# A scheduling priority, 400 instructions ahead, for the recurrence of a hybrid encoder block

## The chip, the cores and the metric

The kernel runs on one core of one Trainium2 chip. The metric is the time of one execution in device microseconds. A core has five engines that this document names: TensorE (PE in the profile, with PEld for its weight loads), VectorE (DVE), ScalarE (ACT), GpSimd (POOL) and SyncE (SP), which here only issues DMAs. Each engine works through its own queue in order; engines wait for each other by semaphores.

## The reference

One encoder layer on a sequence of 1024 tokens, model width 1024, all in float32:

```python
h = rms_norm(x, norm_mix_g)
q, pc, pr = split(h @ w_in)
o = concat([memory_cross_attention(q, mem_n), conformer_conv(pc), rwkv7_bidirectional(pr)])
x = x + o @ w_out
x = x + expert_choice_ffn(rms_norm(x, norm_ffn_g))   # 16 experts, 128 tokens each
y = rms_norm(x, final_norm_g)
```

What matters here is the third group, a recurrence over the tokens with a 64x64 state for each of 6 heads, run once forward and once backward:

```python
def step(state, inp):
    r_t, w_t, k_t, v_t, kk_t, a_t = inp
    sa = einsum('bhij,bhj->bhi', state, -kk_t)
    state = state * w_t[..., None, :] + sa[..., :, None] * (kk_t * a_t)[..., None, :] + v_t[..., :, None] * k_t[..., None, :]
    return state, einsum('bhij,bhj->bhi', state, r_t)
```

## The kernel before, in words

The program has three parts. Up to some 380 us it multiplies the normed input with `w_in` and does the convolution and the cross-attention. From there to some 840 us runs the recurrence, with the first five eighths of the product with `w_out` laid under it (`residual`) and the last part of that product and of the router behind it (`out56`, `partial`). From 860 us on come the experts, which this change does not touch.

The recurrence is cut into chunks of 64 tokens. Six units u = 0 to 5 follow each other: three pairs of heads, two halves each, and a unit holds 8 chunk steps for both directions and both heads of a pair at once. For each unit three things are prepared before its chain can run:

- `prep` (L775) makes the decayed keys and queries (tiles AR, BK): on DVE L801 to L826, on ACT L793 to L814.
- `within` (L845) multiplies them chunk by chunk into the tiles AM (PE L854, masked on DVE at L857).
- `invert` (L887) inverts a triangular matrix per chunk. ACT copies AM into Ld (L895), DVE turns it (L900), and then 31 rounds of two DVE instructions each, L910 (dtmp) and L911 (Dt), depend on one another in a row. After that DVE turns the result back (L916, Dr), ACT and DVE make TT of it (L921, L922), DVE turns a part once more (L926, D), PE multiplies (L934), ACT copies (L938, W), PE multiplies (L945), ACT copies (L949). Then TT is ready.

`chain` (L954) is the recurrence itself. One step of it goes round four engines: PE multiplies the state S0 and the values SV into psX (L969, L971), DVE copies that to Xs (L973), PE multiplies it with TT into psSA (L981), DVE and ACT copy half of that each into SV (L982, L983), PE multiplies into psS (L988), and DVE adds two products into the next state (L991, twice). POOL makes the decayed old state (L965, sps). Beside that PE adds eight products per step to the outputs psY (L976, L996). The first step of unit u needs TT of unit u, at L981, and the state that unit u-1 left.

What sets the order is a generator planner, `run` (L224), that interleaves the functions as the program is recorded, and behind it a scheduler that fills each engine's queue: where several instructions are ready for an engine, the one recorded earlier goes first. The planner's windows (R_INV, R_P and the like, L60 to L93) put `invert`, `prep` and `within` of unit u+1 between the steps of chain u.

Of the kernel before, what the change touches and what calls it, by code (L numbers as in the profile page):

```python
# [12 lines left out]
F32 = mybir.dt.float32  # L13
# [3 lines left out]
ALU = mybir.AluOpType  # L17
# [3 lines left out]
P = 128  # L21
# [10 lines left out]
C = 64  # L32
# [22 lines left out]
FL = [0, 0, 0, 0, 0, 0, 0, 0]  # L55
# [28 lines left out]
NBOR = 0  # L84
PLACE = [11, 2, 3, 4, 5, 6, 7, 8, 1, 9, 10, 0]
NYE = 1
GT = 5
R_O56 = [-3, 36]
R_G2 = [-3, 22]
# [11 lines left out]
def hybrid_block_kernel(ctx: ExitStack, tc: tile.TileContext, x, xT, memT, memn, w_in, w_mk, w_mv, pcols,  # L101
                        ups, gate_up, w_out, g_ffn, g_fin, w_router, w_eg, w_eu, w_ed, out, dbg=None):
    nc = tc.nc
    V, A, G, T = nc.vector, nc.scalar, nc.gpsimd, nc.tensor
# [116 lines left out]
    def mm(tagp="mm", w=512, shape=None, name="mm", bufs=None):  # L221
        return psums[-1].tile(shape or [P, w], F32, name=name, tag=tagp, bufs=bufs or mmb[0].get(tagp))
# [80 lines left out]
    for k in range(KT):  # L303
        h = hp.tile([P, S], F32R, name=f"hh{k}")
        l = hp.tile([P, S], F32R, name=f"hl{k}")
        for n in range(2):
# [5 lines left out]
                                   op1=ALU.subtract)  # L312
# [285 lines left out]
    def attention():  # L598
        assert "kv" in ready
        for hp2 in range(2):  # L600
            for n in range(2):
                pT = at.tile([P, 4, 512], F32, name="pT", tag="pT", bufs=1)
                for jj in range(4):
# [48 lines left out]
    Z = {}  # L652
# [69 lines left out]
    lo, hi = slice(0, 64), slice(64, 128)  # L722
# [229 lines left out]
    state = [None]  # L952

    def chain(p, k, g):  # L954
        AR, BT, SV, TT, pcs = (g[n] for n in ("AR", "BT", "SV", "TT", "pcs"))
        TT = TT.rearrange("p (d c) a b -> p d c (a b)", d=2)
        if k == 0:
            state[0] = Z["sp"].tile([P, 2, C], F32, name="S0", bufs=3)
            V.memset(state[0], 0.0)
        Y = [mm(f"y{d}", shape=[P, HC, C], name="psY", bufs=1) for d in range(2)]  # L960
        for cc in range(HC):
            S0 = state[0]
            AM, c4 = [g["AM", d, cc // 4] for d in range(2)], cc % 4
            sps = Z["sp"].tile([P, 2, C], F32, name="sps", bufs=2)
            G.tensor_mul(sps, S0, pcs[:, :, cc:cc + 1].to_broadcast([P, 2, C]))  # L965
            X = mm("cx", shape=[P, 2, C], name="psX", bufs=2)
            for d in range(2):
                for h, r_, w_ in ((0, lo, hi), (1, hi, lo)):
                    T.matmul(X[w_, d], lhsT=AM[d][r_, c4, h, 0, :], rhs=SV[r_, d, cc, h, :], start=True, stop=False)  # L969
                for r_, w_ in ((lo, hi), (hi, lo)):  # L970
                    T.matmul(X[w_, d], lhsT=AR[r_, d, cc, 0, :], rhs=S0[r_, d], start=False, stop=True)  # L971
            Xs = Z["sp"].tile([P, 2, C], F32, name="Xs", bufs=2)
            (A.copy if FL[3] else V.tensor_copy)(Xs, X)  # L973
            for d in range(2):
                for r_ in (lo, hi):
                    T.matmul(Y[d][r_, cc], lhsT=S0[r_, d], rhs=AR[r_, d, cc, 1, :], start=True, stop=False)  # L976
            yield
            SA = mm("cx", shape=[P, 2, C], name="psSA", bufs=2)
            for d in range(2):
                for r_ in (hi, lo):  # L980
                    T.matmul(SA[r_, d], lhsT=TT[r_, d, cc], rhs=Xs[r_, d], start=True, stop=True)  # L981
            (A.copy if FL[4] else V.tensor_copy)(SV[hi, :, cc, 0, :], SA[hi])  # L982
            (V.tensor_copy if FL[5] else A.copy)(SV[lo, :, cc, 1, :], SA[lo])  # L983
            yield
            S1 = mm("cx", shape=[P, 2, C], name="psS", bufs=2)
            for d in range(2):
                for h, r_ in ((0, lo), (1, hi)):
                    T.matmul(S1[r_, d], lhsT=BT[:, d, cc, h, :], rhs=SV[:, d, cc, h, :], start=True, stop=True)  # L988
            Sn = Z["sp"].tile([P, 2, C], F32, name="S0", bufs=3)
            for d in range(2):  # L990
                V.scalar_tensor_tensor(Sn[:, d], S1[:, d], pcs[:, d, cc:cc + 1], sps[:, d], op0=ALU.mult,  # L991
                                       op1=ALU.add)
            state[0] = Sn
            for d in range(2):
                for h, r_ in ((0, lo), (1, hi)):
                    T.matmul(Y[d][r_, cc], lhsT=SV[:, d, cc, h, :], rhs=AM[d][:, c4, h, 1, :], start=False, stop=True)  # L996
            yield
        Y = [a.rearrange("p a b -> p (a b)") for a in Y]
        if k == 0:
            pair[p]["y"] = Z["sp"].tile([P, S], F32, name="y", bufs=1)  # L1000
        y = pair[p]["y"]
        if k == 0:
            A.copy(y[:, half(0)], Y[0])
            V.tensor_copy(y[:, half(1)][:, ::-1], Y[1])
        else:
            V.tensor_add(y[:, half(1)], y[:, half(1)], Y[0])
            V.tensor_add(y[:, half(0)], y[:, half(0)], Y[1][:, ::-1])
# [381 lines left out]
    for q, op in enumerate((ALU.is_gt, ALU.is_equal)):  # L1389
# [7 lines left out]
             start=True, stop=False)  # L1397
    T.matmul(ps.rearrange("p a b c -> p (a b c)"), lhsT=belowr, rhs=sel.rearrange("p a b c -> p (a b c)"),
             start=False, stop=False)
# [240 lines left out]
```

## Time and profile before

| | |
|---|---|
| Time, median of 3 runs | 1490.68 us (1480.89 to 1491.66) |
| The profiled execution | 1489.13 us |
| its span, first to last instruction | 1487.2 us |
| mean granted TensorE clock | 0.927 |
| PE busy | 1333.4 us, 90% |
| DVE busy | 1216.1 us, 82% |
| ACT busy | 831.2 us, 56% |
| POOL busy | 266.4 us, 18% |

Busy shares are averages over stages with different limits. A matmul's record can reach into the next one's, so a busy PE is not PE at its peak. The clock is a share of full speed, which is 2.4 GHz; the other level is 1.2 GHz. An idle stretch is put down to the engine whose instruction ended the wait.

### The profile page before, as it was taken

To read this page: it belongs to the slowest core of one execution; us is meant where nothing else is said; L and a number is where in the kernel's file an instruction comes from. 1 tells how busy PE (TensorE), PEld (TensorE's weight loads), DVE (VectorE), ACT (ScalarE), POOL (GpSimd) and SP (SyncE) were. 2 spreads that over 40 slices of the span, in tenths; PEclk is the share of its full clock that TensorE was granted. 3 is DMA by queue.
4 is the path that set the end of the run, shared out by engine and by line. 5 is a ranking of instruction groups with operands and counts; after the bars stand their busy time and mean duration, and the time that the engine had idled before them with its cause. 6 is when DMAs were issued, how large, how long until landed. Compare 5 with 4: busy or idle time off the path is not lost.

```text
span 1487.2 us, 24329 instructions
## 1 busy us (share of the span) xinstructions
PE 1333.4 (90%) x9238; PEld 1069.4 (72%) x9238; DVE 1216.1 (82%) x2120; ACT 831.2 (56%) x1214; POOL 266.4 (18%) x238
## 2 busy tenths in 40 slices
PE   6888999997888889888999719999999999999996
PEld 5777667675777776767868618888888887887773
DVE  8899975699686869696833678999999988998886
ACT  4222574433535244434322418888888877887875
POOL 2233322532120312130221000100000110110010
PEclk9999899998898888888999859999999999999998
DMA  8212112422443533342473657999999999999985
GB/s 294 71 61 67 64 64 97 152 71 73 141 143 93 157 97 117 105 121 84 142 272 142 269 198 293 386 393 390 385 385 390 381 379 344 370 377 377 370 302 201
DMA packets 146100, 327.91 MB, mean 220 GB/s; under 512 B 9792, under 2 KB 64960, under 8 KB 145984
## 3 DMA queue, kind: packets, MB, share of 16 engines
q1 hardware_dynamic: 139360, 303.14, 55.6%
q0 software_dynamic: 6192, 22.55, 5.4%
q8 instruction: 72, 1.18, 0.3%
q10 hardware_dynamic: 432, 0.68, 0.1%
q14 instruction: 44, 0.36, 0.1%
HBM read 288.58 MB, written 37.75 MB: 219 GB/s over the span
## 4 chain that ended last, share of the span: by engine, by line
PE 60%; DVE 23%; DMA 6%; ACT 5%; issue 4%; POOL 1%; SPq 0%; POOLq 0%; DVEq 0%; ACTq 0%
PE mm L330 14%; PE mm L331 14%; PE mm L329 14%; DVE cv L517 3%; DVE dtmp L910 2%; DVE Dt L911 2%; DMA fo<-oT_d 2%; PE mm L1435 2%; ACT Ld L895 2%; DMA xk<-in_xT_dram 1%; PE mm L745 1%; PE psA L854 1%; DVE ewl L1354 1%; PE mm L1165 1%; PE mm L1575 1%
## 5 line engine op out<-in xcount | busy, mean ns | idle before, releaser
L1354 DVE SCALAR_TENSOR_TENSOR ewl<-eraw,pc,ewh 128x1024 fp32r<-128x1024 f32 x256 | 315.6, 1280 | 30.5 <-ACT ewh L1353 28.4
L1353 ACT ACTIVATE ewh<-eraw,pc 128x1024 fp32r<-128x1024 f32 x256 | 283.8, 1149 | 31.7 <-PE mm L331 25.7
L330 PE MATMUL mm<-ewl,xh 128*128 128x512 f32 x512 | 202.1, 395 | 3.2 <-DVE ewl L1354 3.0
L331 PE MATMUL mm<-ewh,xl 128*128 128x512 f32 x512 | 200.1, 391 | 0.0
L329 PE MATMUL mm<-ewh,xh 128*128 128x512 f32 x512 | 190.4, 397 | 2.5 <-ACT ewh L1353 2.5
L1350 DVE TENSOR_TENSOR ewl<-eraw,ewh 128x1024 fp32r<-128x1024 f32 x120 | 139.0, 1219 | 2.8 <-ACT ewh L1349 2.8
L329 PE MATMUL mm<-hh,wh 128*128 128x512 f32 x304 | 125.4, 413 | 9.6 <-ACT hh L310 9.6
L1349 ACT ACTIVATE ewh<-eraw 128x1024 fp32r<-128x1024 f32 x120 | 121.6, 1057 | 10.6 <-PE mm L331 9.5
L331 PE MATMUL mm<-hh,wl 128*128 128x512 f32 x304 | 125.5, 413 | 0.8 <-POOL wl L325 0.8
L330 PE MATMUL mm<-hl,wh 128*128 128x512 f32 x304 | 125.1, 412 | 0.9 <-DVE hl L311 0.9
L330 PEld LDWEIGHTS mm<-ewl,xh 128*128 128x128 f32 x512 | 96.6, 189 | 25.8 <-DVE ewl L1354 7.3
L329 PEld LDWEIGHTS mm<-ewh,xh 128*128 128x128 f32 x512 | 96.1, 188 | 23.2 <-ACT ewh L1353 4.2
L331 PEld LDWEIGHTS mm<-ewh,xl 128*128 128x128 f32 x512 | 96.3, 188 | 19.7 <-DVE xl L1438 0.2
L330 PE MATMUL mm<-ewl,fh 128*128 128x512 f32 x240 | 94.6, 394 | 0.3 <-DVE ewl L1350 0.2
L331 PE MATMUL mm<-ewh,fl 128*128 128x512 f32 x240 | 93.6, 390 | 0.0
L329 PE MATMUL mm<-ewh,fh 128*128 128x512 f32 x240 | 88.0, 390 | 0.0
L325 POOL TENSOR_TENSOR wl<-wraw,wh 128x512 fp32r<-128x512 f32 x38 | 58.7, 1548 | 124.5 <-ACT wh L324 83.6
L329 PEld LDWEIGHTS mm<-hh,wh 128*128 128x128 f32 x304 | 59.6, 196 | 25.4 <-ACT hh L310 9.6
L1472 POOL DMA_INDIRECT x_d<-ye,idx x15 | 25.9, 1724 | 283.3 <-ACT ye L1471 283.3
L1420 POOL DMA_INDIRECT xe<-h_d,idx x16 | 28.9, 1805 | 247.0 <-DVE gates L1418 182.3
L517 DVE SCALAR_TENSOR_TENSOR cv<-u,cw,cv 128x512 f32<-128x512 f32 (+1 forms) x87 | 71.5, 853 | 0.1
L330 PEld LDWEIGHTS mm<-hl,wh 128*128 128x128 f32 x304 | 59.1, 194 | 17.4 <-issue 2.7
(417 smaller groups left out, 2950.7 us busy)
## 6 DMA issues: line engine op xcount, KB each, us to landing
eraw<-in_w_eg_dram SPq DMA_DIRECT2D x64, 1024.0 KB, 7.9
eraw<-in_w_eu_dram SPq DMA_DIRECT2D x64, 1024.0 KB, 9.1
eraw<-in_w_ed_dram SPq DMA_DIRECT2D x64, 1024.0 KB, 7.4
fo<-oT_d SPq DMA_DIRECT2D x64, 320.0 KB, 3.9
wraw<-in_w_in_dram SPq DMA_DIRECT2D x38, 256.0 KB, 2.8
ld_k<-d_k SPq DMA_DIRECT2D x18, 256.0 KB, 3.1
ld_v<-d_v SPq DMA_DIRECT2D x18, 256.0 KB, 3.3
xk<-in_xT_dram SPq DMA_DIRECT2D x16, 256.0 KB, 4.7
```

The lines of the kernel that those rows point to most:

```text
L325: G.tensor_sub(wl, raw, wh.bitcast(F32))
L329: T.matmul(ps, lhsT=lh, rhs=rh, start=first, stop=False)
L330: T.matmul(ps, lhsT=lh, rhs=rl, start=False, stop=False)
L331: T.matmul(ps, lhsT=ll, rhs=rh, start=False, stop=last)
L517: V.scalar_tensor_tensor(o[:, 0:ln], z, w, o[:, 0:ln], op0=ALU.mult, op1=ALU.add)
L895: A.copy(Ld[r_, :, c:c + 4].rearrange("p t c -> p c t"), g["AM", d, q][r_, :, h, 0, b * 32:b * 32 + 32])
L910: IE.tensor_tensor(tmp[:, sg, ts], lcol, drow, op=ALU.mult)
L911: IE.tensor_tensor(Dt[:, sg, ts], Dt[:, sg, ts], tmp[:, sg, ts], op=ALU.add)
L1349: A.activation(h, raw[a], AF.Copy)
L1350: V.tensor_sub(l, raw[a], h.bitcast(F32))
L1353: A.activation(h, raw[a], AF.Copy, scale=gain)
L1354: V.scalar_tensor_tensor(l, raw[a], gain, h.bitcast(F32), op0=ALU.mult, op1=ALU.subtract)
```

## The change

Everything that one chain step issues is recorded under a priority 400 instructions ahead of its place. The scheduler then picks a ready chain instruction before any other ready instruction that was recorded up to 400 places earlier. No instruction is added, taken away or changed; the instructions of each engine are the same ones in another order. Three blocks of `chain` are wrapped, with the `yield`s between them:

```diff
+AHEAD = 400
...
         for cc in range(HC):
-            S0 = state[0]
...
+            with tc.high_priority(AHEAD):
+                S0 = state[0]
...
+                (A.copy if FL[3] else V.tensor_copy)(Xs, X)
...
             yield
+            with tc.high_priority(AHEAD):
+                SA = mm("cx", shape=[P, 2, C], name="psSA", bufs=2)
...
             yield
+            with tc.high_priority(AHEAD):
+                S1 = mm("cx", shape=[P, 2, C], name="psS", bufs=2)
...
             yield
```

In the rows of the changed kernel the line numbers are 2 to 5 higher: Xs is L976 there, the SV copy L986, the state L996, Dt L913, the first turn back D L928.

The first place is DVE in unit 0, from the copy Xs of its fourth step on. Before:

```order
L973 COPY Xs<-psX 128x128
L910 TENSOR_TENSOR dtmp<-Lt,Dt 128x8x17
L911 TENSOR_TENSOR Dt<-Dt,dtmp 128x8x17
L910 TENSOR_TENSOR dtmp<-Lt,Dt 128x8x16
L911 TENSOR_TENSOR Dt<-Dt,dtmp 128x8x16
L910 TENSOR_TENSOR dtmp<-Lt,Dt 128x9x15
L911 TENSOR_TENSOR Dt<-Dt,dtmp 128x9x15
L910 TENSOR_TENSOR dtmp<-Lt,Dt 128x9x14
L1089 TENSOR_TENSOR fx<-mm,fx 128x256
L982 COPY SVa<-psSA 64x2x64
```

The same place now, from the same copy Xs on:

```order
L976 COPY Xs<-psX 128x128
L986 COPY SVa<-psSA 64x2x64
L859 TENSOR_TENSOR AM_3006<-psA,mask 128x4x128
L996 SCALAR_TENSOR_TENSOR S_3791<-psS,pcs_1922,sps 128x64 x2
L976 COPY Xs<-psX 128x128
L986 COPY SVa<-psSA 64x2x64
L996 SCALAR_TENSOR_TENSOR S_3907<-psS,pcs_1922,sps 128x64 x2
L976 COPY Xs<-psX 128x128
L986 COPY SVa<-psSA 64x2x64
L1094 TENSOR_TENSOR fx<-mm,fx 128x256
```

Where eight instructions, seven of them of unit 1's inversion, stood between two instructions of the chain, the chain now goes on for nearly three steps with one other instruction between (the mask into AM) and one behind; the inversion of unit 1 (dtmp, Dt) has moved further back.

The second place is PE in unit 0, fifth step, from its product psSA on (mm with fwh, fwl are the residual product, psA is `within`). Before:

```order
L981 MATMUL psSA<-Xs,TT_1939 64x64 x4
L329 MATMUL mm<-fwh,fo_3849 128x256
L330 MATMUL mm<-fwl,fo_3849 128x256
L331 MATMUL mm<-fwh,fo_3850 128x256
...
L331 MATMUL mm<-fwh,fo_3850 128x256
L882 MATMUL mm<-ident,vr 64x64 x16
L988 MATMUL psS<-SVa,BTa 64x64 x4
```

And now, from the psSA of the same step on:

```order
L985 MATMUL psSA<-Xs,TT_1939 64x64 x4
L333 MATMUL mm<-fwh,fo_3373 128x256
L331 MATMUL mm<-fwh,fo_3372 128x256
L332 MATMUL mm<-fwl,fo_3372 128x256
L333 MATMUL mm<-fwh,fo_3373 128x256
L993 MATMUL psS<-SVa,BTa 64x64
```

Between these two products of the chain stood 31 matmuls of other work; now there are four.

The third place is DVE at the end of unit 1's inversion, from the last turn D to the first SV copy of chain 1 (fwl is `residual`). Before:

```order
L926 STREAM_TRANSPOSE D_4027<-TT_3007 128x512
L982 COPY SVa<-psSA 64x2x64
L1077 TENSOR_TENSOR fwl<-fraw,fwh 128x256
L991 SCALAR_TENSOR_TENSOR S_4165<-psS,pcs_1922,sps 128x64 x2
L1004 COPY y<-psY 128x512
L973 COPY Xs<-psX 128x128
L1077 TENSOR_TENSOR fwl<-fraw,fwh 128x256
L857 TENSOR_TENSOR AM_1937<-psA,mask 128x4x128
...
L1077 TENSOR_TENSOR fwl<-fraw,fwh 128x256
L982 COPY SVb<-psSA 64x2x64
```

And now:

```order
L913 TENSOR_TENSOR Dt<-Dt,dtmp 128x16
L918 STREAM_TRANSPOSE Dr<-Dt 128x1024
L1082 TENSOR_TENSOR fwl<-fraw,fwh 128x256 x2
L924 SCALAR_TENSOR_TENSOR TT_3007<-Dr,pm,TT_3007 128x16x32 x2
L928 STREAM_TRANSPOSE D_4027<-TT_3007 128x512
L1082 TENSOR_TENSOR fwl<-fraw,fwh 128x256
L986 COPY SVb<-psSA 64x2x64
```

The last step of chain 0 and the masking for unit 2 have moved ahead of the inversion's end; one instruction is left between the turn D and the first copy of chain 1.

Counted over whole units on DVE, with each instruction counted for itself: from the first SV copy of a chain to its last state there were 140, 124, 178, 134 and 137 instructions in units 0 to 4, and now there are 66, 81, 106, 79 and 90; 31 of each are the chain's own. From there to the next chain's first SV copy there were 9, 15, 4, 10 and 2, and now 95, 56, 80, 61 and 52. Up to the last turn D, of unit 5, 1336 rows stand on DVE in both orders; up to the first product of `normed` behind the recurrence (L1031) PE has the same 4134 matmuls ahead of it in both.

## Rows read from the trace of the kernel before

**Rows 1.** The page, part 2: PE, DVE and the granted clock in 40 slices
```profile
PE   6888999997888889888999719999999999999996
...
DVE  8899975699686869696833678999999988998886
...
PEclk9999899998898888888999859999999999999998
```

**Rows 2.** By unit, then units 0 to 4: engines' busy us, granted clock, DMA share, GB/s
```profile
395.50:465.10 69.60, 60.66 (x831) 51.04 (x830) 57.48 (x151) 26.53 (x55) 11.89 (x13) 0.93 0.44 131
465.10:541.80 76.70, 68.01 (x794) 54.94 (x793) 55.97 (x139) 29.43 (x60) 13.98 (x15) 0.80 0.40 121
541.80:619.40 77.60, 67.55 (x822) 55.06 (x823) 62.87 (x184) 32.74 (x67) 18.31 (x19) 0.85 0.35 108
619.40:691.50 72.10, 62.30 (x809) 50.16 (x810) 57.37 (x144) 28.27 (x59) 13.86 (x15) 0.86 0.36 108
691.50:751.90 60.40, 55.12 (x766) 47.23 (x766) 41.28 (x140) 21.05 (x43) 12.25 (x15) 0.82 0.41 124
751.90:809.10 57.20, 54.43 (x586) 42.76 (x582) 21.12 (x55) 13.41 (x26) 9.82 (x10) 0.98 0.47 186
395.50:751.90 356.40, 313.63 (x4011) 258.44 (x4011) 274.95 (x756) 138.01 (x280) 70.30 (x77) 0.85 0.39 118
```

**Rows 3.** Timeline, DVE, 455 to 466 us (start, us, engine, line)
```profile
456.63 0.70 DVE L926 STREAM_TRANSPOSE D<-TT 128x512 f32<-128x512 f32 x1
...
459.08 0.48 DVE L991 SCALAR_TENSOR_TENSOR S<-psS,pcs,sps 128x64 f32<-128x64 f32 x2 [0.97 <-PE psS L988]
...
465.81 0.29 DVE L982 COPY SVb<-psSA 64x128 f32<-64x128 f32 x1
```

**Rows 4.** Timeline, ACT, the same stretch
```profile
462.01 1.18 ACT L949 COPY TT<-mm 32x512 f32<-32x512 f32 x2
```

**Rows 5.** DVE's groups by line, 395.5 to 751.9 us (busy us, mean ns; idle before)
```profile
L910 DVE TENSOR_TENSOR dtmp<-Lt,Dt 128x56 f32<-128x56 f32 (+22 forms) x155 | 56.8, 366 | 1.8
L911 DVE TENSOR_TENSOR Dt<-Dt,dtmp 128x56 f32<-128x56 f32 (+22 forms) x155 | 51.4, 332 | 2.0
...
L991 DVE SCALAR_TENSOR_TENSOR S<-psS,pcs,sps 128x64 f32<-128x64 f32 x80 | 20.9, 278 | 9.5 <-PE psS L988 9.0
...
L973 DVE COPY Xs<-psX 128x128 f32<-128x128 f32 x40 | 11.4, 285 | 12.5 <-PE psX L971 11.1 <-PE psY L976 1.3
...
L982 DVE COPY SVa<-psSA 64x128 f32<-64x128 f32 x24 | 7.1, 294 | 3.0 <-PE psSA L981 2.5
...
L982 DVE COPY SVb<-psSA 64x128 f32<-64x128 f32 x16 | 4.7, 294 | 2.0 <-PE psSA L981 1.6
```

**Rows 6.** Timeline, DVE: last turn D and the first SV copies of chain 5
```profile
736.85 0.69 DVE L926 STREAM_TRANSPOSE D<-TT 128x512 f32<-128x512 f32 x1
...
752.54 0.29 DVE L982 COPY SVb<-psSA 64x128 f32<-64x128 f32 x1 [1.92 <-PE psSA L981]
...
756.91 0.29 DVE L982 COPY SVb<-psSA 64x128 f32<-64x128 f32 x1 [0.55 <-PE psSA L981]
...
760.65 0.29 DVE L982 COPY SVb<-psSA 64x128 f32<-64x128 f32 x1 [0.57 <-PE psSA L981]
...
763.80 0.29 DVE L982 COPY SVb<-psSA 64x128 f32<-64x128 f32 x1 [0.55 <-PE psSA L981]
...
769.82 0.29 DVE L982 COPY SVb<-psSA 64x128 f32<-64x128 f32 x1
```

**Rows 7.** Who DVE waited for, 395.5 to 751.9 us: total, times, longest
```profile
DVE fx L1089 <- PE mm L331: 17.4, 12, 4.4
...
DVE Lt L900 <- ACT Ld L895: 7.8, 4, 3.9
DVE fb L1020 <- ACT fa L1019: 7.0, 2, 4.0
DVE AM L857 <- PE psA L854: 2.8, 6, 1.0
DVE bonus L842 <- PE mm L753: 2.7, 4, 0.9
```

More of the change, by code (lines that the diff above doesn't have):

```diff
@@ L961, in chain @@
         for cc in range(HC):
-            S0 = state[0]
[L963 to L976, printed above, removed]
-            yield
[L978 to L981, printed above, removed]
@@ L982, in chain @@
-            (A.copy if FL[4] else V.tensor_copy)(SV[hi, :, cc, 0, :], SA[hi])
-            (V.tensor_copy if FL[5] else A.copy)(SV[lo, :, cc, 1, :], SA[lo])
-            yield
[L985 to L996, printed above, removed]
+            with tc.high_priority(AHEAD):
+                S0 = state[0]
+                AM, c4 = [g["AM", d, cc // 4] for d in range(2)], cc % 4
+                sps = Z["sp"].tile([P, 2, C], F32, name="sps", bufs=2)
+                G.tensor_mul(sps, S0, pcs[:, :, cc:cc + 1].to_broadcast([P, 2, C]))
+                X = mm("cx", shape=[P, 2, C], name="psX", bufs=2)
+                for d in range(2):
+                    for h, r_, w_ in ((0, lo, hi), (1, hi, lo)):
+                        T.matmul(X[w_, d], lhsT=AM[d][r_, c4, h, 0, :], rhs=SV[r_, d, cc, h, :], start=True, stop=False)
+                    for r_, w_ in ((lo, hi), (hi, lo)):
+                        T.matmul(X[w_, d], lhsT=AR[r_, d, cc, 0, :], rhs=S0[r_, d], start=False, stop=True)
+                Xs = Z["sp"].tile([P, 2, C], F32, name="Xs", bufs=2)
+                (A.copy if FL[3] else V.tensor_copy)(Xs, X)
+                for d in range(2):
+                    for r_ in (lo, hi):
+                        T.matmul(Y[d][r_, cc], lhsT=S0[r_, d], rhs=AR[r_, d, cc, 1, :], start=True, stop=False)
@@ new lines, in chain @@
+            yield
+            with tc.high_priority(AHEAD):
+                SA = mm("cx", shape=[P, 2, C], name="psSA", bufs=2)
+                for d in range(2):
+                    for r_ in (hi, lo):
+                        T.matmul(SA[r_, d], lhsT=TT[r_, d, cc], rhs=Xs[r_, d], start=True, stop=True)
+                (A.copy if FL[4] else V.tensor_copy)(SV[hi, :, cc, 0, :], SA[hi])
+                (V.tensor_copy if FL[5] else A.copy)(SV[lo, :, cc, 1, :], SA[lo])
+            yield
+            with tc.high_priority(AHEAD):
+                S1 = mm("cx", shape=[P, 2, C], name="psS", bufs=2)
+                for d in range(2):
+                    for h, r_ in ((0, lo), (1, hi)):
+                        T.matmul(S1[r_, d], lhsT=BT[:, d, cc, h, :], rhs=SV[:, d, cc, h, :], start=True, stop=True)
+                Sn = Z["sp"].tile([P, 2, C], F32, name="S0", bufs=3)
+                for d in range(2):
+                    V.scalar_tensor_tensor(Sn[:, d], S1[:, d], pcs[:, d, cc:cc + 1], sps[:, d], op0=ALU.mult,
+                                           op1=ALU.add)
+                state[0] = Sn
+                for d in range(2):
+                    for h, r_ in ((0, lo), (1, hi)):
+                        T.matmul(Y[d][r_, cc], lhsT=SV[:, d, cc, h, :], rhs=AM[d][:, c4, h, 1, :], start=False, stop=True)
```

## The prediction

> **What bounds the kernel now.** I read the page first, for where anything can change at all. In the 40 slices of some 37 us each, the chain runs in slices 11 to 22 (382 to some 800 us), where PE shows 7 to 9, DVE 5 to 9 and the clock 8 or 9 [rows 1]. Neither engine is full there, so I cut that part by unit, from one chain's first SV copy to the next one's [rows 2]. Units 0 to 4 take 356.4 us together, 60 to 78 us each. PE is busy for 313.6 us of them, DVE for 275.0 us. That leaves DVE 356.4 - 275.0 = 81.4 us and PE 42.8 us of idle time: two engines that wait for each other in turn, and no single full one.
>
> Who gates the next unit? The timeline at the turn from unit 0 to 1 shows it [rows 3, 4]: chain 0 writes its last state at 459.1 us, but the first SV copy of chain 1 comes only at 465.8 us. Between them lies the end of unit 1's inversion: the turn D at 456.6 us, two rounds of PE and ACT, and ACT's last copy into TT from 462.0 to 463.2 us. So chain and inversion end at nearly the same time, and the inversion comes last. Its two DVE lines, L910 and L911, are also the largest DVE groups of the stretch, 56.8 and 51.4 us for 155 instructions each; the chain's own instructions make 20.9 + 11.4 + 7.1 + 4.7 = 44.1 us [rows 5].
>
> **The change part by part.** It adds and removes nothing; it moves chain instructions ahead. By the order, a unit on DVE now falls into two parts that alternate: a chain phase (66, 81, 106, 79, 90 instructions in units 0 to 4) and a rest (95, 56, 80, 61, 52), in which most of the next inversion stands. The next chain still needs that inversion, and the number of rows ahead of the last inversion's turn D is unchanged. A faster chain alone therefore gains nothing before unit 5; what counts is whether DVE idles more or less on its way there.
>
> *Work.* The same instructions cost the same, taken at their own times in the trace. The first SV copy of chain 0 now stands 12 DVE rows earlier, and as much work has moved behind it (some 5 us): the start is earlier by what the stretch is longer. Nil.
>
> *Idle time in the chain phases.* How long a step takes with little between its instructions, the trace shows in unit 5, where its first four steps, from 752.54 to 769.82 us, have 26 to 30 PE rows each: 17.28 / 4 = 4.3 us; the two quickest take 3.75 and 3.15 us [rows 6]. In units 0 to 4 a step now has 30 to 40 PE rows. I take 4.3 us, so a chain phase is 8 x 4.3 = 34.4 us (it is 8.9 us a step now, 356.4 / 40). DVE's work in these phases, each instruction at the time its twin took in the trace, is 18, 31, 30, 26 and 26 us. Idle: 16.4 + 3.4 + 4.4 + 8.4 + 8.4 = 41 us. With one mean for all that is not the chain's, (275.0 - 44.1) / (756 - 160) = 0.387 us, the work would be 5 us more a unit and the idle time 29 us, 12 less [rows 2, 5]; I keep the first, since many short pieces stand in the phases, and keep the second for the range.
>
> *Idle time at the handover.* From the turn D to the next chain's first SV copy it is 465.8 - 456.6 = 9.2 us now; to the last copy into TT 463.2 - 456.6 = 6.6 us [rows 3, 4]. The last steps of the old chain used to fill that; by the order one instruction or none is left there in units 1 to 4. I take 7.5 us, between the two and nearer to the lower since the old chain is out of the way on PE and ACT, less 1.1 us of work: 4 x 6.4 = 26 us. At the last handover 20 instructions stand there, some 4.5 us of work, which leaves 3 us.
>
> *Other waits of DVE* do not hang on the chain: for residual products, Ld, fa, psA and bonus 17.4 + 7.8 + 7.0 + 2.8 + 2.7 = 37.7 us [rows 7]. In the chain phases they lie inside the idle time counted above. The rest holds 45, 25, 36, 30 and 18 us of work at the same reckoning, 153 of 283 us. I keep 45% of the waits: 17 us. The bounds are 0 (all of them fall into chain phases) and 37.7.
>
> *Unit 5* takes 57.2 us to the first product of `normed`, with PE busy for 54.4 of them [rows 2]; the same matmuls stand ahead of that product in both orders, with the chain's now first. At most 2.8 us of idle PE can go, and as much can come when the chain's waits lose their cover: nil.
>
> *POOL, ACT and SP.* POOL's sps moves along with the chain. ACT and SP keep their work; ACT is busy for 138.0 of 356.4 us [rows 2], so I put its changed order at nothing.
>
> The sum: 41 + 26 + 3 + 17 = 87 us of idle DVE against 81.4 us, so +6 us. On the profiled execution's 1489.1 us that is 1495; the median of the runs lies 1.6 us above it, and I forecast 1496 us.
>
> **The rivals.** *Two regimes that no longer cover each other (slower).* Mechanism: the rest is now an inversion alternating with `prep`, `within` and `residual` instructions, and each that waits for PE or ACT holds the inversion behind it, with no chain work to pass the time. Then all 37.7 us of other waits stay in the rest, 21 more than I kept, and the handover is 9.2 us as now, 4 x 1.7 = 7 us more: 1496 + 28 = 1524 us. It decides from the point where the waits in the rest exceed some 26 us, which is 1505 us. For it: the first phase of unit 0 holds 18 us of DVE work and 45 us come after. Against: the prep chain's ACT part has had a whole chain phase to run ahead. The Trainium skill has a rule that speaks for this rival (Perfetto Trace Analysis, Optimization Strategy): a kernel whose most-contended engine changes over time may gain by interleaving its regimes. The trace agrees as far as it goes: the kernel before interleaves them and has both engines at 77% to 88%; by the rule alone the separated phases should cost time.
>
> *The chain at its floor (faster).* Mechanism: with the chain first, its steps run as the two quickest of unit 5, at (3.75 + 3.15) / 2 = 3.45 us, a phase is 27.6 us, and DVE's idle time there is 9.6 + 0 + 0 + 1.6 + 1.6 = 13 instead of 41 us: 1496 - 28 = 1468 us. For it: the granted clock is 0.98 in unit 5, where the chain already has little beside it, and 0.80 to 0.93 in units 0 to 4 [rows 2]. Against: units 0 to 4 have more PE rows a step than unit 5 has in these two, and unit 5's mean is 4.3 us. The Trainium skill says that an array that idled is throttled and that activity releases it (TensorE: Matmul & The Clock Gate, What's actually happening); the clocks by unit agree, but no run here shows which way the new order turns them.
>
> *Work-bound (no change).* The wait time only changes its place: PE has 42.8 us of idle time to take up whatever is moved, and the inversion's end stays where its DVE rows put it. 1490 us. For it: the equal row counts up to the last turn D and up to `normed`. Against: the idle time has to come out equal by chance. That the change does nothing at all is excluded by the order.
>
> **How the numbers follow.** About 1%, 15 us, is what a measurement of this kernel can tell from no change. My forecast, with its own spread of some 9 us either way, gets 0.38, work-bound 0.15, the two regimes 0.30, the chain at its floor 0.17. Both of the first lie within 1% (1476 to 1506 us): 0.53. Slower by over 1% is the two regimes: 0.30. Faster by over 1% is the floor: 0.17. The range goes from 1472 us, most of the way to the floor's 1468, to 1520 us, most of the way to the two regimes' 1524; it leaves about 0.1 out on either side. The forecast's own range is 1487 to 1505.
>
> **What would show it.** Right, if in the changed kernel a step of units 0 to 4 takes 4 to 4.7 us from SV copy to SV copy, DVE idles in chain phases, above all in unit 0, and is nearly full in the rests; if the handovers are 7 to 8 us with DVE idle; if the last turn D, at 736.9 us now [rows 6], comes within 10 us of that. The first rival shows in a rest where DVE's waits for PE and ACT add up to over 26 us; the second in steps of 3.5 us and a clock near 1.0 in units 0 to 4. Wrong altogether, if units 0 to 4 lose over 20 us because the work inside them became shorter, or if the experts' part, which I hold to be untouched, changes its length.

## The result, and the profile after

The changed kernel takes 1575.18 us (median of 4 runs, 1567.87 to 1587.32) beside 1491.17 us for the kernel before (1480.89 to 1492.61): ratio 1.0601, 95% interval 1.0557 to 1.0644. It is 84 us slower; the forecast was 1496 us and the range ended at 1520. The profiled execution took 1572.16 us, its span is 1570.1 us. Some executions of a version here ran over 1.5% longer than its fastest one, at a lower clock; the times and ratios here and below are those of the others.

First the page, part 2, of the changed kernel, for [rows 1]:

```profile
PE   6988999997987979697989963999999999999996
...
DVE  8899966787584758777653267999999998999886
...
PEclk9998999995985878888677885999999999999998
```

The clock row is the one that changed most: a 5 in slice 13 (471 to 510 us), a 7 in slice 15, 6 and 7 in slices 20 to 22, where the kernel before has 8 and 9. (The 5 in slice 10, 353 to 393 us, lies ahead of the chain, which starts at the same time as before.) Next the stretch of the chain by unit, cut at the first SV copies as in [rows 2] (engines' busy time in us, then the granted clock, DMA share, GB/s); the last two rows are units 0 to 4 together, and unit 5 up to the last product ahead of the experts:

```profile
395.10:487.80 92.70, 75.35 (x878) 62.53 (x878) 61.38 (x161) 31.10 (x65) 12.08 (x13) 0.85 0.36 108
487.80:574.30 86.50, 73.26 (x793) 57.87 (x792) 53.76 (x137) 26.27 (x52) 15.05 (x15) 0.72 0.34 103
574.30:664.80 90.50, 75.18 (x843) 60.07 (x843) 67.28 (x186) 33.67 (x69) 20.05 (x19) 0.82 0.28 88
664.80:741.20 76.40, 63.97 (x780) 50.23 (x780) 56.16 (x140) 27.34 (x57) 14.41 (x15) 0.86 0.36 107
741.20:817.20 76.00, 68.34 (x775) 55.04 (x775) 43.35 (x142) 24.32 (x50) 12.77 (x15) 0.72 0.36 108
395.10:817.20 422.10, 356.10 (x4064) 285.75 (x4065) 281.93 (x766) 142.70 (x291) 74.36 (x77) 0.80 0.34 102
817.20:918.20 101.00, 97.41 (x725) 74.55 (x724) 31.70 (x84) 20.74 (x39) 14.35 (x21) 0.79 0.43 166
```

The same last stretch of the kernel before:

```profile
751.90:835.60 83.70, 79.97 (x734) 64.46 (x731) 31.63 (x84) 20.67 (x39) 14.27 (x21) 0.95 0.53 206
```

Units 0 to 4 take 422.1 us in place of 356.4, the last stretch 101.0 in place of 83.7: 65.7 + 17.3 = 83 us, the whole loss. What follows, the experts, takes 651.9 us and took 651.6. So read the two stretches from PE. Of a stretch, PE is idle for a part; its busy time times the granted clock is what its work would take at full clock; what is left is the price of the low clock:

| | PE idle | busy x clock | low clock |
|---|---|---|---|
| units 0 to 4, before | 42.8 | 313.6 x 0.85 = 266.6 | 47.0 |
| units 0 to 4, after | 66.0 | 356.1 x 0.80 = 284.9 | 71.2 |
| last stretch, before | 3.7 | 80.0 x 0.95 = 76.0 | 4.0 |
| last stretch, after | 3.6 | 97.4 x 0.79 = 77.0 | 20.5 |

(The clock stands to 0.01 in the rows, so the second and third columns are good to some 2 us. It is the mean of the whole stretch; taken over PE's busy time alone, the low clock of units 0 to 4 is some 5 us more in either kernel, and the difference the same.) Of the 83 us, 23 are idle PE, 19 are work of PE that was not there before, and 41 are the low clock. The matmuls of the program are the same ones, those of the stretch are not quite: the rows of units 0 to 4 hold 4064 here and 4011 before, and 34 of the 53 more are products psA of `within` (292 and 258), which before ran ahead of the first SV copy. At 0.12 us each (12 psA in 1.50 us, below) the 53 are some 6 of the 18 us of added work in units 0 to 4.

The idle part that grew is mostly at the handovers. Who PE waited for in units 0 to 4 of the changed kernel (us, times, longest), and the same wait before:

```profile
PE mm L936 <- DVE D L928: 22.4, 4, 8.8
```
```profile
PE mm L934 <- DVE D L926: 3.6, 2, 2.0
```

PE's timeline at the turn from unit 0 to 1 shows one of the four: it had nothing after the products psA at 471.1 us until the turn D came.

```profile
469.50 0.28 PE L333 MATMUL mm<-fwh,fo 128*128 128x256 f32 x1
469.63 1.50 PE L856 MATMUL psA<-ARb,BK 128*128 128x128 f32 x12
479.90 1.92 PE L936 MATMUL mm<-D,AM 32*32 32x32 f32 x64 [8.77 <-DVE D L928]
```

And the clock through that handover, in windows of 2 us (columns as above):

```profile
470.00:472.00 2.00, 1.12 (x11) 0.93 (x9) 2.00 (x9) 0.55 (x2) 0.00 (x0) 1.00 0.53 122
472.00:474.00 2.00, 0.00 (x0) 0.00 (x0) 1.93 (x6) 0.00 (x0) 0.00 (x0) 1.00 0.70 209
474.00:476.00 2.00, 0.00 (x0) 0.00 (x0) 0.72 (x2) 0.80 (x3) 0.00 (x0) 0.62 0.80 246
476.00:478.00 2.00, 0.00 (x0) 0.00 (x0) 1.36 (x3) 2.00 (x2) 0.00 (x0) 0.50 0.36 116
...
500.00:502.00 2.00, 2.00 (x24) 1.54 (x22) 1.72 (x5) 1.10 (x2) 0.00 (x0) 0.50 0.00 0
...
514.00:516.00 2.00, 2.00 (x39) 1.64 (x40) 1.67 (x5) 0.59 (x2) 1.92 (x2) 0.64 0.05 19
516.00:518.00 2.00, 2.00 (x34) 1.73 (x28) 1.77 (x4) 0.57 (x1) 1.59 (x2) 1.00 0.68 217
```

It falls from 2.4 to 1.2 GHz while PE is idle and stays there until 515 us, through the first half of chain 1 (488.8 to 539.6 us). Of the windows of 1 us in units 0 to 4, 155 lie at the lower level, 95 before. The two other longest stretches at that level, in chain 4 and in chain 5, have no such idle time ahead of them:

```profile
754.00:782.00 28.00, 28.00 (x282) 22.83 (x281) 17.23 (x63) 3.97 (x9) 4.57 (x7) 0.51 0.22 68
816.00:846.00 30.00, 29.27 (x212) 18.98 (x212) 7.18 (x21) 4.58 (x9) 6.28 (x6) 0.50 0.75 283
```

From 740 to 754 us PE was idle for at most 1.2 us at a time, from 800 to 816 us for at most 1.4 us. At half the clock these two stretches of 57 busy us cost some 28 us, so the handovers are not all of the low clock; what let it fall there is open.

On DVE, the lines that answer to [rows 5], with the idle time ahead of them:

```profile
L912 DVE TENSOR_TENSOR dtmp<-Lt,Dt 128x56 f32<-128x56 f32 (+22 forms) x155 | 58.5, 378 | 2.4
L913 DVE TENSOR_TENSOR Dt<-Dt,dtmp 128x56 f32<-128x56 f32 (+22 forms) x155 | 50.5, 326 | 2.3
...
L996 DVE SCALAR_TENSOR_TENSOR S<-psS,pcs,sps 128x64 f32<-128x64 f32 x80 | 19.0, 279 | 20.4 <-PE psS L993 19.5 <-PE psY L1001 0.3
L976 DVE COPY Xs<-psX 128x128 f32<-128x128 f32 x40 | 11.5, 288 | 23.3 <-PE psX L974 22.6 <-PE psY L979 0.4
L986 DVE COPY SVa<-psSA 64x128 f32<-64x128 f32 x24 | 7.1, 295 | 24.4 <-PE psSA L985 24.1
```

The instructions cost what they did (109.0 us for the inversion's two lines, 108.2 before). What grew is the wait of the chain's copies for PE: 9.5 to 20.4 us for the state, 12.5 to 23.3 for Xs, 3.0 to 24.4 for SVa; the last holds handovers too (longest wait 7.8 us).

### The profile page after: what moved, and what is told of

Read it like the earlier page. It is cut to its first block, busy times and chain, and to the rows that moved or that the text cites. A ratio compares the mean times of both kernels' runs of the same rounds, so it can differ in the third digit from the quotient of the medians.

```text
span 1570.1 us, 24322 instructions
## 1 busy us (share of the span) xinstructions
PE 1394.9 (89%) x9238; PEld 1105.4 (70%) x9238; DVE 1220.2 (78%) x2120; ACT 831.5 (53%) x1214; POOL 271.1 (17%) x238
## 4 chain that ended last, share of the span: by engine, by line
PE 63%; DVE 19%; DMA 7%; issue 5%; ACT 4%; POOL 1%; SPq 0%; POOLq 0%; DVEq 0%; ACTq 0%
PE mm L333 14%; PE mm L331 14%; PE mm L332 13%; DVE cv L519 3%; DMA fo<-oT_d 3%; PE psA L856 2%; PE psS L993 2%; DVE dtmp L912 2%; PE mm L1440 2%; DVE Dt L913 2%; PE psX L972 1%; PE psY L1001 1%; PE mm L747 1%; PE psSA L985 1%; PE mm L1170 1%
## 5 line engine op out<-in xcount | busy, mean ns | idle before, releaser
L968 POOL TENSOR_TENSOR sps<-S,pcs 128x128 f32<-128x128 f32 x48 | 21.3, 445 | 300.5 <-DVE S L996 234.9
L912 DVE TENSOR_TENSOR dtmp<-Lt,Dt 128x126 f32<-128x126 f32 (+22 forms) x186 | 70.5, 379 | 3.3
```

Of the source, the lines that this page charges most:

```text
L912: IE.tensor_tensor(tmp[:, sg, ts], lcol, drow, op=ALU.mult)
```

## The experiments

Fifteen further kernels ran. The first four were built on two theories: A, PE runs dry in the handovers, the clock falls and the next chain pays for it; B, the time is lost on VectorE, where the chain's latency lies open and the inversion comes late. The traces of those four gave theory C its reason: each change of TensorE's tile shape has a price. Times are medians; all ratios are against the kernel before, run on the same chip.

For units 0 to 4 (first SV copy of chain 0 to that of chain 5), one row for each run; a change of shape is counted wherever, in PE's timeline, the tile shape (128*128, 64*64, ...) differs from the row before; in e1, e7, e8, e9 and e13 the extra matmuls are in it:

| run | ratio (95% interval) | length | changes | PE idle | busy x clock | low clock |
|---|---|---|---|---|---|---|
| before | 1 | 356.4 | 304 | 42.8 | 266.6 | 47.0 |
| after | 1.0601 (1.0557 to 1.0644) | 422.1 | 362 | 66.0 | 284.9 | 71.2 |
| e1_warm | 1.0676 (1.0617 to 1.0735) | 430.9 | 393 | 39.1 | 352.6 | 39.2 |
| e2_unit5_only | 1.0098 (1.0055 to 1.0141) | 350.4 | 305 | 43.5 | 267.0 | 39.9 |
| e3_ahead40 | 1.0461 (1.0420 to 1.0501) | 409.8 | 531 | 33.5 | 308.5 | 67.7 |
| e4_inversion_too | 1.0422 (1.0368 to 1.0476) | 424.3 | 414 | 50.3 | 291.7 | 82.3 |
| e5_ahead0 | 1.0574 (1.0474 to 1.0673) | 405.0 | 525 | 27.2 | 298.5 | 79.3 |
| e6_counter_runs_on | 1.0488 (1.0423 to 1.0553) | 408.1 | 350 | 64.4 | 278.4 | 65.3 |
| e7_shapes_apart | 1.0437 (1.0368 to 1.0506) | 399.4 | 544 | 24.7 | 314.7 | 60.0 |
| e8_shapes_together | 1.0216 (1.0154 to 1.0277) | 376.0 | 369 | 34.3 | 290.4 | 51.3 |
| e9_warm_short | 1.0513 (1.0455 to 1.0571) | 415.7 | 393 | 42.0 | 321.4 | 52.3 |
| e10_copies_400 | 1.0169 (1.0124 to 1.0213) | 375.4 | 317 | 55.2 | 269.0 | 51.2 |
| e11_products_400 | 1.0329 (1.0263 to 1.0396) | 389.6 | 376 | 43.9 | 283.5 | 62.2 |
| e12_copies_100 | 1.0079 (1.0045 to 1.0113) | 365.2 | 321 | 45.5 | 271.8 | 48.0 |
| e13_counter_warm | 1.0400 (1.0345 to 1.0454) | 415.2 | 383 | 38.2 | 316.6 | 60.3 |
| e14_residual_sticks | 1.0048 (1.0019 to 1.0078) | 352.2 | 289 | 44.1 | 265.0 | 43.1 |
| e15_copies_10 | 1.0042 (1.0008 to 1.0077) | 353.2 | 303 | 44.9 | 268.2 | 40.1 |

**Fill the handovers.** From the changed kernel; a small tile is written in round 26 of the inversion, and matmuls that read it go into the psum tile of the first SA, which the real product overwrites:

```diff
+            if j == WARM_J and g["u"]:
+                gt = g["gate"] = Z["ew"].tile([P, C], F32, name="gate", bufs=1)
+                G.memset(gt, 0.0)
+                G.tensor_copy(gt[:, 0:1], Dt[:, 0, j + 1:j + 2])
...
+                if cc == 0 and "gate" in g:
+                    for _ in range(WARM_N):
+                        T.matmul(SA[lo].rearrange("p a b -> p (a b)"), lhsT=g["gate"], rhs=ident, start=True, stop=True)
```

> The changed kernel, with 56 extra matmuls (about 0.12 us each at full clock, 7 us) on PE in each of the five handovers, just ahead of the inversion's own matmuls; they wait for round 26 of the inversion, so they run in the 5 to 9 us in which PE stood idle. Theory A (PE's idle time in the handover drops the granted clock to 0.5, and the next chain phase runs on that): the chain phases of units 1, 2 and 4, 49.0, 42.7 and 42.0 us in the changed kernel, fall to 32 to 37 us, the clock over units 1 to 4 rises from 0.78 to above 0.9, and the time falls from 1575 to 1530 to 1545 us. Theory B (the chain's latency and the late inversion cost the time, the clock is a by-product): the clock may rise, but the stages keep their lengths, 86, 90, 76 and 76 us, to within 4 us each, and the time stays at 1565 to 1585 us.

Measured 1581.53 us. The mean clock of units 0 to 4 rose from 0.80 to 0.90, and the chain phases of units 1 and 2 fell from 50.8 and 45.7 to 39.2 and 34.1 us, both at a clock of 1.00 (that of unit 4 did not: 43.0 us at 0.68, though its handover was filled). The time did not fall, it lies in theory B's interval. But an extra matmul took 0.22 us, not 0.12, so 280 of them made 62 us and held the inversion's own matmuls back: the first handover lasted 12.5 us in place of 9.7. So theory A is right on the clock of units 1 and 2, and on the time this run cannot decide; it was repeated with half as many, below.

**The priority for unit 5 alone**, recorded for `g["u"] == 5` only.

> The priority for the chain of unit 5 alone; units 0 to 4 are recorded as in the kernel before. Of the 83 us lost up to the last product before the experts, 66 us came in units 0 to 4 and 17 us behind unit 5's first copy into SV. Theory A: the 17 us are the low clock that the last handover left (0.66 in the chain phase), and without an idle PE ahead of it unit 5 costs what it did before: 1486 to 1494 us. Theory B: unit 5's order itself, chain first and the products of the sixth and seventh eighth behind it, costs the 17 us: 1503 to 1510 us.

Measured 1496.46 us, between the two. Its profiled execution, 1488.2 us, has units 0 to 4 6 us shorter and the rest 6 us longer than before. Its chain 5 ran at a clock of 1.00, and the last stretch took 89.3 us with PE idle for 4.3 us (745.3 to 834.6 us, clock 0.92). So unit 5's order by itself costs some 6 of the 17 us in this one execution; the other 11 are seen only in the changed kernel, at its lower clock (0.79).

**A lead of 40:** `AHEAD = 40`.

> The changed kernel with a lead of 40 instructions in place of 400: chain phases of 143, 120, 174, 120 and 137 DVE instructions and rests of 13, 21, 10, 25 and 4, nearly those of the kernel before. Both theories: the cost comes from the separation into phases, so no stage loses over 4 us and the time is 1480 to 1500 us. Rival: the lead itself exposes the chain's waits whatever its length; then a part of the 84 us, 20 or more, is there already: over 1510 us.

Measured 1558.99 us: theories A and B both fail, the rival's time holds. VectorE's phases are nearly those of before, PE waits for D only 7.7 us, and units 0 to 4 still lose 53 us. The row of units 0 to 4 says where:

```profile
392.15:801.94 409.79, 376.25 (x4030) 297.73 (x4031) 272.17 (x762) 140.44 (x286) 69.41 (x77) 0.82 0.35 106
```

PE is idle for 33.5 us, less than before, and busy 62.6 us longer with nearly the same matmuls (4030 and 4011): 42 us of it are work at full clock, 21 the low clock. In PE's timeline the tile shape changes 531 times where it changed 304 times.

**The inversion ahead as well:** each step of `invert` under the same priority.

> The changed kernel with the inversion also recorded 400 instructions ahead, so that it is picked before prep, within and the residual product again: rests of 93, 22, 52, 28 and 39 DVE instructions in place of 95, 56, 80, 61 and 52. Theory A: the turn D comes earlier, PE has fill work left for the handover, its waits for D fall from 22.4 us to under 8 us, and with them the low clock: 1490 to 1530 us. Theory B, too, gains from the earlier inversion, but only by the DVE idle time of the handovers (5 x 5 us): 1545 to 1560 us with the clock of the phases still below 0.85.

Measured 1556.18 us, a ratio 0.018 (27 us) below the change and above theory A's interval. The wait for D fell to 6.0 us as expected of theory A, but in units 0 to 4 PE's work and the low clock grew by more than the idle time shrank (424.3 us in place of 422.1): 414 changes of shape, a clock of 0.78. What came back lies behind unit 5's first copy, in a stretch of 90.5 us at a clock of 0.92, where the change has 101.0 at 0.79. The time is in theory B's interval, but theory B wanted a clock of the phases still below 0.85, and three of the five phases have 0.98, 0.89 and 1.00. So no theory fits this run, and as the inversion's lead changed TensorE's order too, it does not show what closed handovers are worth alone.

**A lead of 0:** `AHEAD = 0`.

> The changed kernel with a lead of 0. The context restores the priority counter when it closes, so what is recorded behind a chain block gets the same numbers as the block; the scheduler then takes the two by turns. By the order DVE's phases are those of the kernel before (140, 131, 177, 130 and 137 instructions, rests of 5 to 11), but TensorE changes its tile shape (128x128, 128x64, 64x128, 64x64, 32x32) 506 times in units 0 to 4, where the kernel before does so 294 times, and 131 times in the chain of unit 5 (before 42). Theory C (each change of shape costs TensorE some 0.15 us at full clock and 0.2 to 0.25 at half, a fit to the rows of six timelines): 212 x 0.18 = 38 us in units 0 to 4 and up to 16 behind them, 1515 to 1550 us. Theory A (PE idle in the handovers drops the clock): no handover opens, 1480 to 1500 us.

Measured 1568.25 us, longer than even theory C had it, and as slow as the change itself, with no lead at all. So something other than the lead is at work, and it is the counter: the context gives the instructions inside it their numbers, and on closing sets the counter back to where it was on entering. What is recorded next gets the same numbers again, and the scheduler takes a chain block and the fill work behind it in turn. Units 0 to 4:

```profile
397.05:802.05 405.00, 377.79 (x4009) 300.51 (x4009) 276.84 (x756) 138.22 (x280) 73.05 (x77) 0.79 0.35 108
```

PE is busy for 93% of the stretch. The 221 further changes of shape go with 298.5 - 266.6 = 32 us more work, 0.14 us each.

**A lead of 400 with the counter running on:**

```diff
-            with tc.high_priority(AHEAD):
+            with ahead_of():
...
+        def __exit__(self, *e):
+            q = tc.cur_priority
+            self.h.__exit__(*e)
+            tc.cur_priority = q + AHEAD
```

> A lead of 400 in which the counter runs on behind each block, as if the block had been recorded at its place: 338 changes of tile shape in units 0 to 4 (294 before, 350 in the changed kernel), 50 in the chain of unit 5 (42, 66), and phases still apart: 91, 81, 111, 81 and 94 DVE instructions in a chain phase, 71, 57, 76, 60 and 49 in a rest. Theory A: phases apart leave the handovers open, the clock falls as in the changed kernel, 1540 to 1575 us. Theory C: 44 changes at 0.18 us, 8 us, and as much again for opened handovers: 1495 to 1515 us.

Measured 1556.57 us: theory A's interval, not C's. Only 46 changes more than before, but PE waits for D 18.5 us, is idle for 64.4 us, and its clock is 0.81. The two ways to lose are separate: no handovers and many changes in e5, open handovers and few changes here. What the set-back counter adds at a lead of 400 is 1.0601 - 1.0488, some 17 us.

**The price of a change by itself.** On the kernel before, matmuls that add zero to the residual product's sum (the 64x64 block of `ident` off its diagonal is zero):

```diff
                 for k in range(5):
                     mm3(ps, o[0][:, k], o[1][:, k], wh[:, k], wl[:, k], k == 0, k == 4)
+                    for _ in range(EXTRA[k]):
+                        T.matmul(ps[lo, 0:C], lhsT=ident[lo, hi], rhs=ident[lo, lo], start=False, stop=False)
```

with `EXTRA = (1, 1, 1, 1, 0)`, and `(4, 0, 0, 0, 0)` for the same matmuls side by side.

> The kernel before, with four extra 64x64 matmuls in each of the residual product's accumulations, which add zero to it; here they stand apart, one behind each of the first four groups of three products. 532 changes of tile shape in units 0 to 4; with the same four matmuls side by side 357. Theory C: 175 changes at 0.15 to 0.25 us, 26 to 44 us more TensorE time than with the four together, of which the 43 us in which PE idles may take up a part: 15 to 40 us longer than the run with the four together. Against it (a change of shape is free, only the number of matmuls counts): the two runs within 5 us.

> The kernel before, with the four extra 64x64 matmuls side by side behind the first three products of each accumulation: 357 changes of tile shape in units 0 to 4, 63 more than before. Theory C: 63 x 0.18 = 11 us and 4 us for the 120 matmuls themselves, 1492 to 1506 us; against it: 1488 to 1494 us.

Measured 1548.03 and 1516.17 us: 31.9 us for the same matmuls in another place, and 544 - 369 = 175 changes, 0.18 us each. (The two profiled executions lie 23.1 us apart, 1535.17 and 1512.07 us, which makes 0.13.) Units 0 to 4 of the run apart, and of the run together:

```profile
399.73:799.14 399.41, 374.70 (x4254) 293.89 (x4254) 272.23 (x754) 135.33 (x275) 73.73 (x77) 0.84 0.35 106
```
```profile
399.66:775.67 376.01, 341.68 (x4254) 281.67 (x4255) 273.86 (x753) 136.01 (x276) 74.61 (x77) 0.85 0.36 110
```

The number of matmuls is the same, 4254, and PE is busy 33 us longer. In PE's timeline, at full clock, apart (each extra matmul shows as two records):

```profile
401.68 0.38 PE L332 MATMUL mm<-fwh,fo 128*128 128x256 f32 x1
401.99 0.33 PE L1091 MATMUL mm<-ident 64*64 64x64 f32 x2
402.25 0.39 PE L330 MATMUL mm<-fwh,fo 128*128 128x256 f32 x1
402.47 0.28 PE L331 MATMUL mm<-fwl,fo 128*128 128x256 f32 x1
402.59 0.28 PE L332 MATMUL mm<-fwh,fo 128*128 128x256 f32 x1
402.80 0.33 PE L1091 MATMUL mm<-ident 64*64 64x64 f32 x2
```

and together:

```profile
401.87 0.38 PE L332 MATMUL mm<-fwh,fo 128*128 128x256 f32 x1
402.19 0.67 PE L1091 MATMUL mm<-ident 64*64 64x64 f32 x8
402.79 0.38 PE L330 MATMUL mm<-fwh,fo 128*128 128x256 f32 x1
403.01 0.28 PE L331 MATMUL mm<-fwl,fo 128*128 128x256 f32 x1
403.13 0.28 PE L332 MATMUL mm<-fwh,fo 128*128 128x256 f32 x1
403.25 0.28 PE L330 MATMUL mm<-fwh,fo 128*128 128x256 f32 x1
```

Read the starts. Three products in a row take 0.36 us (403.13 + 0.12 for each). Apart, three products and one extra take 402.80 - 401.99 = 0.81 us, so one extra matmul with two changes costs 0.45. Together, three products and four extras take 403.13 - 401.87 = 1.26 us, so four with two changes cost 0.90. The difference is three matmuls: 0.15 each, and a change is (0.45 - 0.15) / 2 = 0.15 us. The same two distances are 0.81 us as the median of 56 places at full clock in the run apart and 1.26 us of 11 in the run together. It is the shape, and not another operation, that has the price: from a product to psA, both 128*128, the start comes 0.13 us later (469.50 to 469.63, in the timeline of the handover above), between two products 0.12; from a product to the 64*64 one 0.21 us (402.59 to 402.80). That the run together came out longer than expected is the matmuls' own 0.15 us, which I had put at 0.03.

**The filling again, shorter:** `WARM_N` 28 in place of 56, on the changed kernel and on the one with the running counter.

> As the run with 56 extra matmuls in each handover, with 28: those took 0.22 us each, so 12.4 us a handover where 5 to 9 us were idle, and pushed the inversion's own matmuls back; 28 take 6.2 us and fit. Theory A (the clock that falls in the handover is part of the loss of the changed kernel): units 0 to 4 take 398 to 410 us (422 in the changed kernel, 431 with 56), the half clock 80 to 110 of them (155 in the changed kernel), and with the chain of unit 5 some 10 us shorter the time is 1535 to 1556 us. Against it: 1565 to 1585 us.

> The lead of 400 with the counter running on (1557 us) and 28 extra matmuls in each handover, as in the run with the short filling. 371 changes of tile shape in units 0 to 4, 44 in the chain of unit 5. If the clock that falls in the handovers is a part of its own in the loss, it comes back here as it did in the changed kernel: half clock in 90 to 115 us of units 0 to 4 (137 without), 1535 to 1552 us. If the gain in the changed kernel was only a matter of where its products stood, 1553 to 1565 us.

Measured 1559.96 us, a ratio 0.009 (13 us) below the change, and 1550.6 us, likewise 0.009 below e6; the half clock stands for 109 and 124 us. The first time misses theory A's interval by 4 us and lies under the one against it, the second is in theory A's. The intervals of the ratios overlap with those of the runs without filling, but the gain came out the same twice; of the expected clock the first got its share, the second did not. The row of units 0 to 4 of the first:

```profile
392.93:808.65 415.72, 373.75 (x4337) 306.05 (x4338) 281.17 (x766) 141.75 (x289) 78.04 (x86) 0.86 0.35 105
```

Against the changed kernel 24 us of idle PE and 19 us of low clock are gone, but the filling is 140 x 0.22 = 31 us of work and brought 31 changes of shape: 6 us are left there, and 5 more came behind unit 5's first copy. So the idle handover is a cause of the low clock, since work in it brings part of the clock back, but not the only one, and work that serves for nothing else barely pays for itself.

**The change in halves**, on the kernel before, with a running counter: the copies and VectorE's products, and the matmuls.

```diff
-            (A.copy if FL[3] else V.tensor_copy)(Xs, X)
+            with lead(LEAD_C):
+                (A.copy if FL[3] else V.tensor_copy)(Xs, X)
...
+            with lead(LEAD_P):
+                for d in range(2):
+                    for r_ in (hi, lo):
+                        T.matmul(SA[r_, d], lhsT=TT[r_, d, cc], rhs=Xs[r_, d], start=True, stop=True)
```

> The kernel before with the lead of 400 for the chain's copies, products on VectorE and the one on GpSimd alone, TensorE's products left at their place, the counter running on. 302 changes of tile shape in units 0 to 4 (294 before), 41 in the chain of unit 5; chain phases of 136, 102, 154, 111 and 138 DVE instructions, rests of 13, 37, 32, 31 and 3. Theories A and C: nothing on TensorE's side has changed but one handover or two, 1478 to 1500 us. Theory B (what the chain is put ahead of on VectorE comes late, the inversion above all): 1505 to 1540 us.

> The other half: the lead of 400 for TensorE's products alone, copies left at their place, the counter running on. 369 changes of tile shape in units 0 to 4, 48 in the chain of unit 5; phases of 129, 126, 177, 131 and 107 DVE instructions, rests of 31, 11, 11, 8 and 39, so handovers open before units 1 and 5 alone. Theory C: 75 x 0.18 = 14 us, and theory A two handovers of 8 us and the low clock behind them, 10 to 20 us: 1505 to 1535 us. Theory B: without the copies ahead VectorE's order is nearly that of before, 1485 to 1495 us.

> The copies alone with a lead of 100: 303 changes of tile shape in units 0 to 4, 41 in the chain of unit 5; phases of 139, 115, 168, 113 and 138 DVE instructions. Theories A and C: 1475 to 1495 us, and if the copies' shorter waits on VectorE are worth anything, below the kernel before. Theory B: between the kernel before and the lead of 400 for the copies, 1495 to 1515 us.

Measured 1511.72, 1533.1 and 1500.09 us. The halves add up: 0.0169 + 0.0329 = 0.0498 against 0.0488 for both (e6). The copies alone leave PE's work as it was (269.0 against 266.6 us), but VectorE takes the chain first, the inversion ends later than PE's fill lasts, and PE's wait for D grows from 3.6 to 14.2 us: theory B's interval, by theory A's handover. The matmuls alone bring 72 changes, 17 us of work and 15 us of low clock, in theory C's interval. The lead of 100 came out in theory B's interval as well, 5 us above the other.

**Two tries for a faster kernel:** on the kernel before, residual accumulations that stay together once begun (`with lead(400)` around the last twelve products), and the copies with a lead of 10.

> The kernel before with the last twelve of the fifteen products of each residual accumulation 400 ahead, the counter running on, so that an accumulation once begun is finished: 282 changes of tile shape in units 0 to 4 (294 before), 42 in the chain of unit 5. By 0.15 to 0.25 us a change it gains 2 to 3 us, against it stands that the chain's products wait up to 2 us more behind an accumulation: 1482 to 1494 us. If the number of changes alone counted, 1483 to 1487 us.

> The kernel before with a lead of 10 for the chain's copies alone, the counter running on: TensorE's tile shapes change 294 and 42 times as before, VectorE's phases are 141, 125, 177, 130 and 137 instructions with rests of 9, 16, 5, 15 and 3. No handover opens and no change of shape is added: 1480 to 1494 us. If leads of the copies cost by themselves, as 12 us at 100 and 25 us at 400 might say, 1494 to 1500 us.

Measured 1495.49 us (ratio 1.0048, 1.0019 to 1.0078), just above its interval though 15 changes fewer were counted, and 1493.02 us (1.0042, 1.0008 to 1.0077), inside the first. Neither beats the kernel before; no version that ran does.

## Why the prediction was wrong

By its own steps:

- **Work, nil** is the step that failed: "The same instructions cost the same, taken at their own times in the trace". It held on DVE (281.9 us for 766 instructions against 275.0 for 756) and was never worked out for PE, whose busy time grew by 42.5 us in units 0 to 4: 18 us of work at full clock and 24 us of low clock. I took PE's 42.8 us of idle time as its reserve and counted rows, when what a matmul costs depends on its neighbours and on the clock. Of the 18 us, 58 further changes of shape at 0.15 us are 9, and some 6 are the 53 matmuls that only moved into the stretch; the other 3 are within what the rounded clock leaves open.
- **Idle time in the chain phases**, 8 x 4.3 = 34.4 us each. The first phase took 33.7 us, at a clock of 1.00: the term was right where its condition held. The others took 50.8, 45.7, 38.5 and 42.8 us, 5.3 us a step over all five, and DVE was idle for 74.7 us in them, not 41. The duration of a step was read in unit 5 at a clock of 0.98 [rows 2, 6] and carried to phases whose clock was 0.66 to 0.87. In e1, where the phases of units 1 to 3 had a clock of 0.97 to 1.00, they took 39.2, 34.1 and 34.9 us.
- **The handover**, 26 + 3 us of idle DVE. From turn D to first SV copy it was 9.7, 8.5, 8.6, 7.8 and 17.4 us, and DVE was idle for 41.6 us. The four were 1 us longer each than the 7.5 I took; the last was missed, and the last turn D came at 800.4 us, 64 us later than before, where the prediction allowed 10. What was missed altogether is that PE is idle there too, waiting for the same turn D: 22.4 us.
- **Other waits**, 17 us in the rests: measured 22.8 us outside the handovers, inside the bounds. The three together: 139 us of idle DVE against the 87 forecast, 34 of the 52 missing ones in the chain phases.
- **Unit 5, nil:** 17.3 us longer, 16.5 of them the low clock (0.79 in place of 0.95) by the table of the result; to the first product of `normed`, the prediction's own cut, 76.0 us in place of 57.2. The filled handovers bring 5 of them back (95.7 us at 0.87 in the run with 28 matmuls), though no idle stretch over 1.4 us stands ahead of this fall of the clock. That the number of matmuls ahead of `normed` is unchanged was true and beside the point.
- **POOL, ACT and SP, nil**, and the experts untouched: right (ACT 142.7 against 138.0 us, the experts 651.9 against 651.6).
- **Sums.** Three readings were loose, none enough to matter: in slices 11 to 22 PE shows 8 to 9 and DVE 3 to 9; with one mean for the other instructions the work is 3 us more a unit, not 5; and 153 of 283 us is 54%, so by its own share 20 us of the other waits stay, not 17.
- **The rivals.** The two regimes had the direction and, in the handover, a part of the mechanism, but their place was wrong: the rests held 22.8 us of such waits, under the 26 from which they were to decide, and 84 us were lost in place of 28. The chain at its floor counted on a higher clock and got a lower one. "That the change does nothing at all is excluded by the order" was right; that it does only what its words say was not: I took the lead to move the chain alone, and the counter that is set back renumbers everything behind it. At a lead of 0 that by itself costs some 85 us, at 400 some 17.

The Trainium skill has the rule that I passed over (TensorEngine Tiling (Array Packing), Tiling Modes): changing the tiling mode drains TensorE. The runs agree and give the price that it does not name, 0.15 us a change at full clock. On the clock (TensorE: Matmul & The Clock Gate, What's actually happening) the Trainium skill says that an idle array is throttled and that activity releases it. The fall of the clock in the handover at 471 to 480 us agrees; of the release the trace shows less, since PE was busy by the profile for 33.1 of the 34.1 us from 479.9 to 514.0 us and the clock stayed at 1.2 GHz.

What stays open is the larger part of the low clock, the largest of the three losses. It is shown behind an idle handover in units 1 and 2; in chains 4 and 5 it fell without one, and in e5 the low clock costs 79 us, 32 more than before, though PE idles less there (27.2 us). No run changed the clock alone. Why the last handover took 17.4 us was not followed up either.

## What to carry to other kernels

Before a priority or another reorder is costed, count on TensorE how often its tile shape changes in the new order, and price each change; equal instruction counts say nothing about that. Where two alternating kinds of work are pulled apart, ask for each engine, not only for the one thought to be the bound, what it still has to do in the gap between them, and what its clock does afterwards. And look at what a scheduling context does to the instructions behind it: the lead of 0 is the control that shows it.

## What the runs showed of the hardware

- A change of TensorE's tile shape costs 0.15 us at full clock by the rows above (0.18 us by the times of two kernels, 0.13 by their profiled executions); a 64x64 float32 matmul among 128x128 ones, with its two changes, 0.45 us for 0.15 us of work. The profile shows this time as busy: 33 us more in the run apart than in the run together, with 4254 matmuls in both.
- After an idle stretch of 8.8 us the granted clock stayed at 1.2 GHz from 475 to 515 us, though PE was busy for all 2.00 us of the window at 500 us; chain 1, 33 us of it on that clock, took 50.8 us, where chain 0 took 33.7 at a clock of 1.00.
- It fell without a long idle stretch too: from 754 to 782 us PE was busy throughout at 1.2 GHz, and in the 14 us before that it was idle for at most 1.2 us at a time.
- Work put into the idle stretches raised the mean clock of units 0 to 4 from 0.80 to 0.86 (28 matmuls each) and 0.90 (56).
